# Odd mixer of a hybrid decoder step: four gate rows, and decay rows spread over the partitions by TensorE

## The chip, the cores and the metric

The kernel runs on one core of one Trainium2 chip. The metric is the device time of one execution in microseconds; lower is better. Three runs of the kernel before took 1924.58 to 1926.36 us, with a median of 1924.73 us.

## The reference, cut to what matters

Two decoder layers are applied to a prompt of 512 tokens and a sample group of 8 x 4 = 32 tokens, which share all weights (width 1024). Each layer is a SwiGLU half-step, a mixer and a second SwiGLU half-step. The change lies in the mixer of the second layer, a gated DeltaNet with 8 heads of width 128. Per head it does this (chunks of 64 tokens in the reference, of 128 in the kernel, which gives the same result):

```
q, k, v = silu(causal_conv(u @ w_in));  q, k = l2_normalize(q) * 128**-0.5, l2_normalize(k)
g = -exp(A_log) * softplus(a_logit + dt_bias);  G = cumsum(g)            # per head and token, within a chunk
decay = exp(where(s <= t, G[t] - G[s], -inf))                           # chunk x chunk
A = where(s < t, (k_t . k_s) * decay, 0) * beta_t;   P = (q_t . k_s) * decay
(I + A) [Uv, Wk] = [v * beta, k * beta * exp(G)]                        # unit lower triangular
for each chunk:  U = Uv - Wk S;  O = (q exp(G)) S + P U;  S = exp(G_last) S + (k exp(G_last - G))^T U
o = rms_norm(O, o_gain) * silu(z);   x = x + o @ w_out
```

The decay needs G twice: down the partitions (one value for each token of a row) and along the free axis, the same row of 128 values on every partition. The second form is what the change makes in another way. The "gate" is silu(z).

## The kernel before, in words

Activations are kept transposed: 8 tiles of 128 features x 544 tokens (512 of the prompt, 32 of the sample). A linear layer (`mm3`, L347) splits weights and activations each into a rounded part and a rest, and runs three matmuls for each 128 x 128 block of weights (L362 to L364), for the first 256 tokens and then for the other 288. One such pair of halves takes about 6 us of TensorE. Its results go to one of two PSUM buffers, in turn, and VectorE or another engine clears each before it can be used again.

In the odd mixer (L1499) the order of the work is written out by hand in `ODD_ORDER`: D decays of a group of two heads, H query and key of a head, B its values, V the triangular solve (62 small VectorE instructions, one after the other, L1223 and L1224), L the larger blocks of the inverse (`levels`), C the recurrence over the chunks (`chain`), S and R the sample group, Z a gate, O, M and U the output layer, N the convolution states:

```
ODD_ORDER = "D0 H0 H1 B0 B1 V0 Z0 L0 Z1 S0 C0 R0 D2 H2 B2 H3 B3 Z2 Z3 V2 L2 D4 S2 C2 R2 H4 H5 B5 D6 Z4 B4 V4 Z5 H6 S4 H7 B6 L4 V6 C4 R4 B7 Z6 O0 Z7 S6 N L6 C6 R6 M2 O6"
```

This order is a priority and not the final sequence: when the kernel is built, a planner puts the instructions of each engine into one fixed order, by that priority and its own estimate of when each is ready. It also hands out the buffers of each tile pool: a tile that finds all buffers of its tag taken waits for the last reader of one of them. On the chip every engine then works through its own list in order.

The steps that the change touches:

- `odd_setup` (L1008) computes G for all heads. It forms the cumulative sums by matmuls with constant matrices (L1042 to L1046), turns G on its side (`gt`, 40 rows x 128: row 8c+h is chunk c of head h, rows 32 to 39 are the sample's; L1072) and stores `gt` in DRAM (`gdr`, five DMAs, L1074 and L1075). The sample's rows come back on all 128 partitions in one DMA (`grs`, L1077).
- `head_decay` (L1128) loads a head's row of G on all partitions (`grow`, or `E.xsq` for the second head of a group; L1132) and makes the two decay matrices Dn and Dt, four VectorE instructions each (L1137, L1138), and their exponentials on ScalarE. `sample_decay` (L1351) does the same for the sample from `grs`.
- `head_stage` (L1146) transposes q and k into PSUM (tag "m", two buffers), squares each on ScalarE for the norms with the squares going to a scratch tile `E.junk` (L1158, L1164), copies k to the tile `kt` (L1165), makes A (L1177, into Dn) and P (L1184, into Dt), and stores A for the solve. `kt` is requested between the squares of q and the transposes of k.
- The tiles Dn, Dt, kt, qg and vb of all heads share the tag "st", which has 15 buffers: ten for a group of two heads.
- `chain` (L1281) and `sample_group` (L1368) also square into `E.junk` (L1335, L1383).
- `gate` (L1529) runs the linear layer of silu(z) for one head; VectorE clears it into a tile `sz` (L1537), which has three buffers. The gate is read when the chain ends (L1307, L370, L371).
- `odd_consts` (L969) loads the constant matrices during the FFN before the mixer.

Of the kernel before, what the change touches and what calls it, by code (L numbers as in the profile page):

```python
# [7 lines left out]
F32 = mybir.dt.float32  # L8
# [7 lines left out]
P = 128  # L16
D = 1024
T = 512
# [950 lines left out]
def odd_consts(E, op):  # L969
    nc, I = E.nc, E.I  # L970

    def const(key, shape):
        t = op.tile(shape, F32, name=key)
        nc.sync.dma_start(out=t, in_=I[key])
        return t
    E.tri = const("c_tri", [P, P])
    E.mba = const("c_mba", [P, P])
    E.mbp = const("c_mbp", [P, P])
    E.stri = const("c_stri", [NS, NS])
    E.sones = const("c_sones", [NS, NS])  # L980
    E.smba = const("c_smba", [NS, NS])
    E.smbp = const("c_smbp", [NS, NS])
    E.bsel = const("c_bsel", [96, DB])

    rows = E.f(P)[:96]
    nc.sync.dma_start(out=rows, in_=I["dn_conv_w"].rearrange("a i (k p) -> (a i k) p", p=P))
    ps = E.m([P, 96])
    nc.tensor.transpose(ps, rows, E.ident[:96, :96])
    E.cw = op.tile([P, 96], F32, name="cw")
    nc.vector.tensor_copy(E.cw, ps)  # L990
    E.cst = op.tile([P, 24, 27], F32, name="dncst")
    cv = I["state_dn_conv"].rearrange("a b i c -> (a b i) c")
    for g in range(6):
        st = E.f()
        nc.sync.dma_start(out=st[:24, :512], in_=cv[:, g * 512:(g + 1) * 512])
        ps = E.m([P, 4, 24])
        for j in range(4):
            nc.tensor.transpose(ps[:, j], st[:24, j * P:(j + 1) * P], E.ident[:24, :24])
        nc.vector.tensor_copy(E.cst[:, 4 * g:4 * g + 4, 3:], ps)
    gc = op.tile([P, 1], F32, name="ogain")  # L1000
    nc.sync.dma_start(out=gc, in_=I["dn_o_gain"].rearrange("a p -> p a"))
    E.ogain = gc
    E.ad = op.tile([P, 2, NH], F32, name="ad")
    nc.sync.dma_start(out=E.ad[:, 0], in_=I["dn_A_log"].to_broadcast([P, NH]))
    nc.sync.dma_start(out=E.ad[:, 1], in_=I["dn_dt_bias"].to_broadcast([P, NH]))


def odd_setup(E, op, sp, w_in):  # L1008
# [5 lines left out]
    def ev(h, c0, cn, ps):  # L1014
        nc.vector.tensor_tensor(bt[:16, c0:c0 + cn], ps[:16], E.rstd[:16, c0:c0 + cn], op=ALU.mult)
    mm3(E, [w], E.xh, E.xl, ev)
    ps = E.m([P, 5, 16])
    for t, (c0, n) in enumerate(TOKS):
        nc.tensor.transpose(ps[:n, t], bt[:16, c0:c0 + n], E.ident[:16, :16])
# [19 lines left out]
    nc.vector.tensor_tensor(gm, g[:NS, 4:5].to_broadcast([NS, DB, NH]), bc(E.bsel[:NS], NH), op=ALU.mult)  # L1039
    ps = E.m([P, 160])  # L1040
    gf = g[:, :4].rearrange("p a b -> p (a b)")
    nc.tensor.matmul(ps[:, 0:32], lhsT=E.tri, rhs=gf, start=True, stop=True)  # L1042
    nc.tensor.matmul(ps[:, 32:64], lhsT=E.ones, rhs=gf, start=True, stop=True)
    nc.tensor.matmul(ps[:NS, 64:72], lhsT=E.stri, rhs=g[:NS, 4], start=True, stop=True)
    nc.tensor.matmul(ps[:NS, 72:80], lhsT=E.sones, rhs=g[:NS, 4], start=True, stop=True)
    nc.tensor.matmul(ps[:, 96:160], lhsT=E.ones[:NS], rhs=gm.rearrange("p a b -> p (a b)"), start=True, stop=True)  # L1046
    E.G = op.tile([P, 5, NH], F32, name="G")
    nc.vector.memset(E.G, 0.0)
# [24 lines left out]
    for c in range(4):  # L1073
        nc.sync.dma_start(out=E.gdr[:, c * P:(c + 1) * P], in_=gt[8 * c:8 * c + 8, :P])  # L1074
    nc.sync.dma_start(out=E.gdr[:, T:], in_=gt[32:40, :NS])  # L1075
    E.grs = op.tile([P, NH, NS], F32, name="grs")
    nc.sync.dma_start(out=E.grs, in_=E.gdr[:, T:].unsqueeze(0).to_broadcast([P, NH, NS]))  # L1077


def conv_tile(E, op, w_in, i, h, sq):  # L1080
# [31 lines left out]
def ch(ap):  # L1112
    return ap[:, :T].rearrange("p (c t) -> p c t", c=4)


def cps(E, shape, tag="c"):
    return E.pm.tile(shape, F32, tag=tag, name=E.nm(tag))
# [10 lines left out]
def head_decay(E, op, h):  # L1128
    nc = E.nc
    H = Head()  # L1130
    grow = E.xsq if h % GH else op.tile([P, NT], F32, tag="grow", name=E.nm("grow"))
    nc.sync.dma_start(out=grow, in_=E.gdr[h:h + 1].to_broadcast([P, NT]))  # L1132
    Dn = op.tile([P, 4, P], F32, tag="st", name=E.nm("Dn"), bufs=ST)
    Dt = op.tile([P, 4, P], F32, tag="st", name=E.nm("Dt"), bufs=ST)
    for c in range(4):
        g = E.G[:, c, h:h + 1]
        nc.vector.scalar_tensor_tensor(Dn[:, c], ch(grow)[:, c], g, E.mba, op0=ALU.subtract, op1=ALU.max)  # L1137
        nc.vector.scalar_tensor_tensor(Dt[:, c], ch(grow)[:, c], g, E.mbp, op0=ALU.subtract, op1=ALU.min)  # L1138
    E.act(Dn, Dn, AF.Exp, scale=-1.0)
    E.act(Dt, Dt, AF.Exp)  # L1140
    E.act(grow[:, :T], grow[:, :T], AF.Exp)
    H.grow, H.A, H.PT = grow, Dn, Dt
    return H


def head_stage(E, op, w_in, h, H, ssq, adr, sq):  # L1146

    nc = E.nc
    gi = h % GH
    grow, A, PT = H.grow, H.A, H.PT  # L1150
    qT = conv_tile(E, op, w_in, 0, h, sq)
    kT = conv_tile(E, op, w_in, 1, h, sq)
    ssk = op.tile([P, 4], F32, tag="ssk", name=E.nm("ssk"), bufs=2)
    pq = E.m([P, 4, P])
    for c in range(4):
        nc.tensor.transpose(pq[:, c], ch(qT)[:, c], E.ident)
    for c in range(4):
        nc.scalar.activation(E.junk[0], pq[:, c], AF.Square, accum_out=ssq[:, gi, c:c + 1])  # L1158
    kt = op.tile([P, 4, P], F32, tag="st", name=E.nm("kt"), bufs=ST)
    pk = E.m([P, 4, P])  # L1160
    for c in range(4):
        nc.tensor.transpose(pk[:, c], ch(kT)[:, c], E.ident)
    for c in range(4):
        nc.scalar.activation(E.junk[0], pk[:, c], AF.Square, accum_out=ssk[:, c:c + 1])  # L1164
    nc.scalar.activation(kt, pk, AF.Copy)  # L1165
    nc.vector.tensor_scalar(ssk, ssk, EPS, None, op0=ALU.add)
    cf = op.tile([P, 4, 4], F32, tag="cf", name=E.nm("cf"), bufs=4)
    rk, rb, rb2, kwf = cf[:, 0], cf[:, 1], cf[:, 2], cf[:, 3]
    rsqrt_small(E, rk, ssk, [P, 4], "4")
    nc.vector.tensor_tensor(rb, rk, E.beta[:, :4, h], op=ALU.mult)  # L1170
    nc.vector.tensor_tensor(rb2, rb, rk, op=ALU.mult)
    nc.vector.scalar_tensor_tensor(kwf, rb2, -1.0, E.eG[:, :4, h], op0=ALU.mult, op1=ALU.mult)
    kk = E.m([P, 4, P])
    for c in range(4):
        nc.tensor.matmul(kk[:, c], lhsT=ch(kT)[:, c], rhs=ch(kT)[:, c], start=True, stop=True)
    for c in range(4):
        nc.vector.scalar_tensor_tensor(A[:, c], kk[:, c], rb2[:, c:c + 1], A[:, c], op0=ALU.mult, op1=ALU.mult)  # L1177
    for i in range(4):
        s = slice(32 * i, 32 * i + 32)
        nc.sync.dma_start(out=adr[i, gi].rearrange("c r s -> r c s"), in_=A[s, :, s])  # L1180
    qk = E.m([P, 4, P])
    for c in range(4):
        nc.tensor.matmul(qk[:, c], lhsT=ch(kT)[:, c], rhs=ch(qT)[:, c], start=True, stop=True)
    nc.vector.tensor_tensor(PT, qk, PT, op=ALU.mult)  # L1184
    qg = op.tile([P, 4, P], F32, tag="st", name=E.nm("qg"), bufs=ST)
    nc.gpsimd.tensor_tensor(qg, ch(qT), ch(grow), op=ALU.mult)
    kw = op.tile([P, 3, P], F32, tag="kw", name=E.nm("kw"), bufs=GH)
    for c in range(1, 4):
        nc.scalar.activation(kw[:, c - 1], kt[:, c], AF.Copy, scale=kwf[:, c:c + 1])
    for c in range(4):  # L1190
        nc.scalar.activation(kt[:, c], kt[:, c], AF.Copy, scale=E.egl[:, c, h:h + 1])
    H.qg, H.kg, H.kw, H.rb = qg, kt, kw, rb
# [88 lines left out]
def chain(E, op, Hs, V, g0, ssq, sz, yy, cuts=(4,)):  # L1281
# [29 lines left out]
    for c in range(4):  # L1311
# [20 lines left out]
            nc.tensor.matmul(po[:, h], lhsT=Hs[h].PT[:, c], rhs=U[:, h], start=(c == 0), stop=True)  # L1332
        nc.scalar.activation(ot[:, c], po, AF.Copy)
        for h in hs:
            nc.scalar.activation(E.junk[1], ot[:, c, h], AF.Square, accum_out=sso[:, h, c:c + 1])  # L1335
        S = Sn
        if c in cuts:
            finish(c - 4 // len(cuts), c)
# [29 lines left out]
def sample_group(E, op, sq, dec, g0, sz, yy):  # L1368
# [10 lines left out]
    nc.scalar.activation(kv, ps, AF.Copy)  # L1379
    kt, vt = kv[:, 0], kv[:, 1]  # L1380
    ssk = op.tile([NS, GH], F32, tag="sssk", name=E.nm("ssk"))
    for h in hs:
        nc.scalar.activation(E.junk[1][:NS], kt[:, h], AF.Square, accum_out=ssk[:, h:h + 1])  # L1383
    nc.vector.tensor_scalar(ssk, ssk, EPS, None, op0=ALU.add)
    cf = op.tile([NS, 4, GH], F32, tag="scf", name=E.nm("scf"))
    rk, rb, rb2, kwf = cf[:, 0], cf[:, 1], cf[:, 2], cf[:, 3]
# [26 lines left out]
        nc.tensor.matmul(pv[:, h], lhsT=A2[:, h], rhs=IB[:, h], start=True, stop=True)  # L1413
    V = R(NS, "V")
    nc.vector.tensor_tensor(V, pv, IB, op=ALU.add)
    kw = R(P, "kw")
    nc.vector.tensor_tensor(kw, kt, bc(kwf, P), op=ALU.mult)
    k3 = op.tile([96, GH, P], F32R, tag="k3", name=E.nm("k3"))
    for h in hs:
# [79 lines left out]
def odd_mixer(E, cp, w_in, w_out, nxt):  # L1499
    nc, tc = E.nc, E.tc  # L1500
    with E.phase(0, 2), tc.tile_pool(name=E.nm("oddw"), bufs=1) as op, tc.tile_pool(name=E.nm("odram"), bufs=1, space=bass.MemoryType.DRAM) as dp:
        E.dp, E.op = dp, op
        E.ft, E.rt = (op, "acc", XW, 4), (op, "y", YB)
        E.junk = [op.tile([P, P], F32, name=f"junk{i}") for i in range(2)]
        norm_stats(E)
        odd_setup(E, cp, op, w_in)
        odd_heads(E, op, dp, w_in, w_out, nxt)


def odd_heads(E, op, dp, w_in, w_out, nxt):  # L1510
# [156 lines left out]
```

## Time and profile before

| | us |
|---|---|
| median of the runs (lowest, highest) | 1924.73 (1924.58, 1926.36) |
| the profiled execution | 1924.04 |
| its span in the trace | 1922.3 |
| TensorE busy in the span | 1872.1 |
| VectorE busy | 1080.6 |
| ScalarE busy | 836.6 |
| GpSimd busy | 125.5 |

The profile follows one execution. A row of a timeline has the start in us from the span's start, the duration, the engine (PE TensorE, PEld its weight load, DVE VectorE, ACT ScalarE, POOL GpSimd, SPq the DMA queue of SyncE), the line of the kernel, the operation, output and inputs by tile name, the shape and how many instructions are merged; in brackets the idle time of that engine just before, and what ended it. One fp32 matmul of the kernel appears as two instructions, so "x8" of a 128x128 product are four matmuls. PEclk is the granted clock of TensorE as a share of full speed.

### The profile page before, as it was taken

How to read it: one execution, taken by the hardware profiler on the slowest of the kernel's cores; microseconds unless marked ns; L12 is line 12 of the kernel's file. 1: busy time of each engine (PE TensorE's matmuls, PEld its weight loads, DVE VectorE, ACT ScalarE, POOL GpSimd, SP SyncE). 2: the span in 40 equal slices, each digit the busy share in tenths (PEclk: the TensorE clock that was granted, in tenths of full speed). 3: DMA queues.
4: the chain of work that ended last, by engine and by line, in shares of the span. 5: the costliest groups of instructions: out<-in, count | busy, mean ns of one | idle time of the engine just before them, and what ended most of it. 6: DMA issues, size and time to landing. Idle time of an engine off the chain costs nothing.

```text
span 1922.3 us, 36590 instructions
## 1 busy us (share of the span) xinstructions
PE 1872.1 (97%) x15037; PEld 1792.7 (93%) x15037; DVE 1080.6 (56%) x2563; ACT 836.6 (44%) x1733; POOL 125.5 (7%) x237
## 2 busy tenths in 40 slices
PE   7999999999899999999999999899998999999999
PEld 7999999889768999999999999899998998999998
DVE  7444435786756544433544433688978877444422
ACT  6333324777744433322433322475775646333221
POOL 0000002111320000000000000112111100000000
PEclk9999999999999999999999999999999999999999
DMA  4333233322332333323333332333443332233232
GB/s 134 88 89 89 77 88 104 85 56 78 86 103 84 88 88 88 88 79 88 97 88 88 88 93 78 89 88 83 109 125 76 93 91 69 83 86 88 85 112 68
DMA packets 315972, 171.03 MB, mean 89 GB/s; under 512 B 28470, under 2 KB 310278, under 8 KB 315804
## 3 DMA queue, kind: packets, MB, share of 16 engines
q1 hardware_dynamic: 313244, 160.30, 29.7%
q0 software_dynamic: 2560, 8.39, 1.5%
q8 instruction: 118, 1.93, 0.4%
q14 instruction: 50, 0.41, 0.1%
HBM read 158.01 MB, written 10.65 MB: 88 GB/s over the span
## 4 chain that ended last, share of the span: by engine, by line
PE 84%; DVE 7%; ACT 4%; issue 2%; DMA 2%; POOL 1%; SPq 0%; ACTq 0%; DVEq 0%; POOLq 0%
PE lin L362 25%; PE lin L363 24%; PE lin L364 24%; PE pv L729 1%; DVE wl L324 1%; ACT wh L323 1%; PE sc L758 1%; PE po L805 1%; DMA raw<-in_w_ffn_in 1%; DVE acc L1106 1%; DVE LT L1224 1%; DVE ltmp L1223 1%; PE s L1451 0%; ACT f L100 0%; DMA raw<-in_w_in_odd 0%
## 5 line engine op out<-in xcount | busy, mean ns | idle before, releaser
L362 PE MATMUL lin<-xh,wh 128*128 128x256 f32 (+2 forms) x2992 | 873.8, 292 | 19.5 <-DVE sz L1537 4.5
L363 PE MATMUL lin<-xl,wh 128*128 128x256 f32 (+2 forms) x2992 | 871.1, 291 | 1.1 <-DVE xl L371 1.0
L364 PE MATMUL lin<-xh,wl 128*128 128x256 f32 (+2 forms) x2992 | 865.2, 289 | 0.8 <-DVE wl L324 0.8
L362 PEld LDWEIGHTS lin<-xh,wh 128*128 128x128 f32 (+1 forms) x2992 | 564.7, 189 | 26.7 <-ACT wh L323 8.4
L364 PEld LDWEIGHTS lin<-xh,wl 128*128 128x128 f32 (+1 forms) x2992 | 566.3, 189 | 6.1 <-issue 4.1
L363 PEld LDWEIGHTS lin<-xl,wh 128*128 128x128 f32 (+1 forms) x2992 | 564.9, 189 | 5.3 <-issue 1.7
L323 ACT ACTIVATE wh<-raw 128x1024 fp32r<-128x1024 f32 x261 | 275.8, 1057 | 493.3 <-PE lin L363 425.6
L324 DVE TENSOR_TENSOR wl<-raw,wh 128x1024 fp32r<-128x1024 f32 x261 | 317.4, 1216 | 89.5 <-PE lin L364 87.7
L362 PE MATMUL lin<-hh,wh 128*128 128x288 f32 (+1 forms) x1024 | 295.7, 289 | 0.0
L363 PE MATMUL lin<-hl,wh 128*128 128x288 f32 (+1 forms) x1024 | 295.4, 288 | 0.0
L364 PE MATMUL lin<-hh,wl 128*128 128x288 f32 (+1 forms) x1024 | 294.9, 288 | 0.0
L363 PEld LDWEIGHTS lin<-hl,wh 128*128 128x128 f32 x1024 | 193.0, 188 | 0.2
L364 PEld LDWEIGHTS lin<-hh,wl 128*128 128x128 f32 x1024 | 192.7, 188 | 0.1
L362 PEld LDWEIGHTS lin<-hh,wh 128*128 128x128 f32 x1024 | 192.5, 188 | 0.1
L401 DVE TENSOR_TENSOR sg<-lin,rstd 128x256 f32<-128x256 f32 (+1 forms) x128 | 55.9, 438 | 161.3 <-PE lin L364 161.3
L406 DVE TENSOR_TENSOR pr<-lin,rstd 128x256 f32<-128x256 f32 (+1 forms) x128 | 56.5, 441 | 155.3 <-PE lin L364 155.1
L370 ACT ACTIVATE hh<-pr 128x256 fp32r<-128x256 f32 (+1 forms) x128 | 55.1, 431 | 202.4 <-DVE pr L407 202.2
L423 DVE SCALAR_TENSOR_TENSOR x<-lin,x 128x256 f32<-128x256 f32 x64 | 28.2, 441 | 168.7 <-PE lin L364 168.7
L371 DVE TENSOR_TENSOR hl<-pr,hh 128x256 fp32r<-128x256 f32 (+1 forms) x128 | 56.6, 442 | 62.1 <-ACT hh L370 62.0
L100 ACT ACTIVATE sg<-sg 128x256 f32<-128x256 f32 (+1 forms) x128 | 53.7, 422 | 55.9 <-DVE sg L401 55.9
L267 ACT ACTIVATE xh<-x,vec 128x544 fp32r<-128x544 f32 (+2 forms) x64 | 39.6, 632 | 73.1 <-DVE x L423 59.3
L1106 DVE SCALAR_TENSOR_TENSOR acc<-XP,cw,acc 128x568 f32<-128x568 f32 x72 | 58.9, 818 | 2.1 <-ACT acc L1104 1.8
(480 smaller groups left out, 2091.3 us busy)
## 6 DMA issues: line engine op xcount, KB each, us to landing
raw<-in_w_ffn_in SPq DMA_DIRECT2D x128, 512.0 KB
raw<-in_w_ffn_out SPq DMA_DIRECT2D x64, 512.0 KB
raw<-in_w_in_odd SPq DMA_DIRECT2D x32, 512.0 KB
raw<-in_w_in_even SPq DMA_DIRECT2D x20, 512.0 KB
raw<-in_w_out_even SPq DMA_DIRECT2D x8, 512.0 KB
S<-in_state_dn_S SPq DMA_DIRECT2D x8, 512.0 KB
out_dn_S_sample<-S SPq DMA_DIRECT2D x8, 512.0 KB
raw<-in_w_out_odd SPq DMA_DIRECT2D x8, 512.0 KB
```

The lines of the kernel that those rows point to most:

```text
L100: i = self.nc.scalar.activation(out, in_, func, **kw).ins
L267: nc.scalar.activation(xh, x, AF.Copy, scale=g)
L323: nc.scalar.activation(self.h, raw, AF.Copy)
L324: nc.vector.tensor_tensor(self.l, raw, self.h.bitcast(F32), op=ALU.subtract)
L362: nc.tensor.matmul(ps[:n], lhsT=wh, rhs=rh, start=(i == 0), stop=False)
L363: nc.tensor.matmul(ps[:n], lhsT=wh, rhs=rl, start=False, stop=False)
L364: nc.tensor.matmul(ps[:n], lhsT=wl, rhs=rh, start=False, stop=(i == len(terms) - 1))
L370: nc.scalar.activation(yh, src, AF.Copy)
L371: nc.vector.tensor_tensor(yl, src, yh.bitcast(F32), op=ALU.subtract)
L401: nc.vector.tensor_tensor(s, ps, E.rstd[:, c0:c0 + cn], op=ALU.mult)
L406: nc.vector.tensor_tensor(p_, ps, E.rstd[:, c0:c0 + cn], op=ALU.mult)
L1106: nc.vector.scalar_tensor_tensor(a, XP[:, j:j + XW - 3], cw[j], a, op0=ALU.mult, op1=ALU.add)
```

## The change

Four things are done. The sample's rows of G (`grs`) and the two rows of heads 0 and 1 are spread over the partitions by TensorE: a matmul whose weights are one column of the identity, repeated 128 times, copies one row of `gt` to all partitions. The other heads still load theirs from DRAM. The gates get four buffers in place of three. The scratch tile `E.junk` is gone: squares go to `kt` in `head_stage` (which is therefore requested before the transposes of q), to `vb` in `chain` and to `kw` in `sample_group`. Three constant matrices are loaded in `odd_setup`, into a work tile, and no longer kept from the FFN on.

```diff
 def odd_consts(E, op):
-    E.tri = const("c_tri", [P, P])
-    E.stri = const("c_stri", [NS, NS])
-    E.sones = const("c_sones", [NS, NS])
 def odd_setup(E, op, sp, w_in):
     mm3(E, [w], E.xh, E.xl, ev)
+    cst = E.f()
+    tri, stri, sones = cst[:, :P], cst[:NS, P:P + NS], cst[:NS, P + NS:P + 2 * NS]
+    for t, key in ((tri, "c_tri"), (stri, "c_stri"), (sones, "c_sones")):
+        nc.sync.dma_start(out=t, in_=E.I[key])
...
     nc.sync.dma_start(out=E.gdr[:, T:], in_=gt[32:40, :NS])
     E.grs = op.tile([P, NH, NS], F32, name="grs")
-    nc.sync.dma_start(out=E.grs, in_=E.gdr[:, T:].unsqueeze(0).to_broadcast([P, NH, NS]))
+    row = lambda r: E.ident[:40, r:r + 1].to_broadcast([40, P])
+    ps = cps(E, [P, NH, NS], "s")
+    for h in range(NH):
+        nc.tensor.matmul(ps[:, h], lhsT=row(32 + h), rhs=gt[:40, :NS], start=True, stop=True)
+    nc.scalar.activation(E.grs, ps, AF.Copy)
+    E.growps = [cps(E, [P, 4, P], t) for t in ("c", "z")]
+    for h, ps in enumerate(E.growps):
+        for c in range(4):
+            nc.tensor.matmul(ps[:, c], lhsT=row(8 * c + h), rhs=gt[:40, :P], start=True, stop=True)
 def head_decay(E, op, h):
-    nc.sync.dma_start(out=grow, in_=E.gdr[h:h + 1].to_broadcast([P, NT]))
+    if h < GH:
+        src = E.growps[h]
+    else:
+        nc.sync.dma_start(out=grow, in_=E.gdr[h:h + 1].to_broadcast([P, NT]))
+        src = ch(grow)
...
-        nc.vector.scalar_tensor_tensor(Dn[:, c], ch(grow)[:, c], g, E.mba, op0=ALU.subtract, op1=ALU.max)
-        nc.vector.scalar_tensor_tensor(Dt[:, c], ch(grow)[:, c], g, E.mbp, op0=ALU.subtract, op1=ALU.min)
+        nc.vector.scalar_tensor_tensor(Dn[:, c], src[:, c], g, E.mba, op0=ALU.subtract, op1=ALU.max)
+        nc.vector.scalar_tensor_tensor(Dt[:, c], src[:, c], g, E.mbp, op0=ALU.subtract, op1=ALU.min)
-    E.act(grow[:, :T], grow[:, :T], AF.Exp)
+    E.act(ch(grow), src, AF.Exp)
 def head_stage(E, op, w_in, h, H, ssq, adr, sq):
+    kt = op.tile([P, 4, P], F32, tag="st", name=E.nm("kt"), bufs=ST)
     pq = E.m([P, 4, P])
...
-        nc.scalar.activation(E.junk[0], pq[:, c], AF.Square, accum_out=ssq[:, gi, c:c + 1])
-    kt = op.tile([P, 4, P], F32, tag="st", name=E.nm("kt"), bufs=ST)
+        nc.scalar.activation(kt[:, c], pq[:, c], AF.Square, accum_out=ssq[:, gi, c:c + 1])
...
-        nc.scalar.activation(E.junk[0], pk[:, c], AF.Square, accum_out=ssk[:, c:c + 1])
+        nc.scalar.activation(kt[:, c], pk[:, c], AF.Square, accum_out=ssk[:, c:c + 1])
 def chain(E, op, Hs, V, g0, ssq, sz, yy, cuts=(4,)):
-            nc.scalar.activation(E.junk[1], ot[:, c, h], AF.Square, accum_out=sso[:, h, c:c + 1])
+            nc.scalar.activation(Hs[h].vb[:, c], ot[:, c, h], AF.Square, accum_out=sso[:, h, c:c + 1])
 def sample_group(E, op, sq, dec, g0, sz, yy):
+    kw = R(P, "kw")
     for h in hs:
-        nc.scalar.activation(E.junk[1][:NS], kt[:, h], AF.Square, accum_out=ssk[:, h:h + 1])
+        nc.scalar.activation(kw[:, h], kt[:, h], AF.Square, accum_out=ssk[:, h:h + 1])
...
-    kw = R(P, "kw")
 def odd_mixer(E, cp, w_in, w_out, nxt):
-        E.junk = [op.tile([P, P], F32, name=f"junk{i}") for i in range(2)]
     def gate(h):
-        z = op.tile([P, NT], F32, tag="sz", name=E.nm("sz"), bufs=3)
+        z = op.tile([P, NT], F32, tag="sz", name=E.nm("sz"), bufs=4)
```

The matmuls of L1042 to L1045 take `tri`, `stri` and `sones` in place of `E.tri`, `E.stri` and `E.sones`.

## Rows read from the trace of the kernel before

**Rows 1.** Busy time by stretch: the odd mixer (span us, then engines busy, PEclk, DMA).

```profile
1200.00:1640.00 440.00, 418.81 (x3888) 391.65 (x3887) 354.17 (x1231) 269.42 (x760) 61.60 (x128) 0.98 0.35 92
```

**Rows 2.** Timeline of VectorE, first decays.

```profile
1229.44 0.28 DVE L1072 COPY gt<-m 40x128 f32<-40x128 f32 x1 [0.39 <-PE m L1070]
...
1237.83 0.35 DVE L1137 SCALAR_TENSOR_TENSOR Dn<-grow,G,c_mba 128x128 f32<-128x128 f32 x1 [0.25 <-DMA grow<-gdr]
...
1242.76 0.42 DVE L1092 TENSOR_TENSOR XP<-lin,rstd 128x256 f32<-128x256 f32 x1
```

**Rows 3.** Timeline of TensorE, the stretch after.

```profile
1243.32 0.36 PE L362 MATMUL lin<-xh,wh 128*128 128x256 f32 x1 [2.68 <-DVE XP L1092]
```

**Rows 4.** Busy time by stretch after two stalls of TensorE (PEclk is third from last).

```profile
1243.30:1247.20 3.90, 3.88 (x20) 3.90 (x21) 2.69 (x8) 3.35 (x7) 3.09 (x5) 0.58 0.12 22
1452.90:1458.90 6.00, 6.00 (x28) 6.00 (x29) 5.07 (x19) 2.05 (x8) 0.00 (x0) 0.50 0.33 90
```

**Rows 5.** Timeline of TensorE: fp32 matmuls between linear ones, in two places.

```profile
1250.30 1.16 PE L1175 MATMUL m<-acc 128*128 128x128 f32 x8
1251.21 0.38 PE L364 MATMUL lin<-xh,wl 128*128 128x288 f32 x1
...
1490.92 0.40 PE L1464 MATMUL s<-ident,uo 32*128 32x32 f32 x2
1491.16 0.38 PE L1465 MATMUL s<-sPT,Us 32*128 32x32 f32 x2
```

**Rows 6.** Groups of VectorE by line and form: output, input, count, busy us, mean ns.

```profile
L1177 DVE SCALAR_TENSOR_TENSOR Dn<-m,cf,Dn 128x128 f32<-128x128 f32 x32 | 9.1, 343 | 0.0
...
L1137 DVE SCALAR_TENSOR_TENSOR Dn<-xsq,G,c_mba 128x128 f32<-128x128 f32 x16 | 5.5, 346 | 0.6 <-DMA xsq<-gdr 0.6
```

**Rows 7.** Timeline of ScalarE and of SyncE's DMA queue, first decays.

```profile
1235.27 0.77 ACT L1104 ACTIVATE acc<-XP,cw 128x568 f32<-128x568 f32 x1 [5.17 <-DVE XP L1096]
...
1213.24 0.35 SPq L1215 DMA_DIRECT2D LT<-in_c_lid  x1
```

**Rows 8.** Timeline of VectorE and TensorE around the sixth gate.

```profile
1448.71 0.68 DVE L371 TENSOR_TENSOR y<-sz,y 128x512 fp32r<-128x512 f32 x1
...
1452.42 0.41 DVE L1537 TENSOR_TENSOR sz<-lin,rstd 128x256 f32<-128x256 f32 x1
...
1452.89 0.58 PE L362 MATMUL lin<-xh,wh 128*128 128x256 f32 x1 [4.50 <-DVE sz L1537]
```

**Rows 9.** Timeline of ScalarE, keys of heads 7 and 3 (of head 7, first and last square).

```profile
1497.62 0.28 ACT L1164 ACTIVATE junk<-m 128x128 f32<-128x128 f32 x1 [0.70 <-PE m L1162]
...
1499.00 0.19 ACT L1164 ACTIVATION_READ_ACCUMULATOR junk<-m 128x1 f32 x1
...
1510.68 0.60 ACT L1165 ACTIVATE kt<-m 128x512 f32<-128x512 f32 x1 [1.11 <-PE c L1270]
...
1350.64 0.59 ACT L1165 ACTIVATE kt<-m 128x512 f32<-128x512 f32 x1
```

**Rows 10.** Timeline of VectorE: head 3's norm, A of head 7, starts of two solves.

```profile
1337.08 0.15 DVE L956 TENSOR_SCALAR rsi<-ssk 128x4 int32<-128x4 int32 x1
...
1339.73 0.15 DVE L961 SCALAR_TENSOR_TENSOR cf<-rsa,rsy 128x4 f32<-128x4 f32 x1
...
1361.53 0.20 DVE L1223 TENSOR_TENSOR ltmp<-LA,LT 128x31 f32<-128x31 f32 x1
...
1507.12 1.13 DVE L1177 SCALAR_TENSOR_TENSOR Dn<-m,cf,Dn 128x128 f32<-128x128 f32 x4
...
1523.39 0.20 DVE L1223 TENSOR_TENSOR ltmp<-LA,LT 128x31 f32<-128x31 f32 x1
```

**Rows 11.** Timeline of SyncE's DMA queue and TensorE: two solves back, last levels.

```profile
1474.76 2.16 SPq L1242 DMA_DIRECT2D V<-tdr  x4
...
1560.22 2.61 SPq L1242 DMA_DIRECT2D V<-tdr  x4
...
1571.66 0.24 PE L1248 MATMUL c<-ident,V 32*32 32x32 f32 x2
```

More of the change, by code (lines that the diff above doesn't have):

```diff
@@ L1041, in odd_setup @@
     gf = g[:, :4].rearrange("p a b -> p (a b)")
-    nc.tensor.matmul(ps[:, 0:32], lhsT=E.tri, rhs=gf, start=True, stop=True)
+    nc.tensor.matmul(ps[:, 0:32], lhsT=tri, rhs=gf, start=True, stop=True)
     nc.tensor.matmul(ps[:, 32:64], lhsT=E.ones, rhs=gf, start=True, stop=True)
-    nc.tensor.matmul(ps[:NS, 64:72], lhsT=E.stri, rhs=g[:NS, 4], start=True, stop=True)
-    nc.tensor.matmul(ps[:NS, 72:80], lhsT=E.sones, rhs=g[:NS, 4], start=True, stop=True)
+    nc.tensor.matmul(ps[:NS, 64:72], lhsT=stri, rhs=g[:NS, 4], start=True, stop=True)
+    nc.tensor.matmul(ps[:NS, 72:80], lhsT=sones, rhs=g[:NS, 4], start=True, stop=True)
     nc.tensor.matmul(ps[:, 96:160], lhsT=E.ones[:NS], rhs=gm.rearrange("p a b -> p (a b)"), start=True, stop=True)
```

## The prediction

> **What bounds the kernel now.** I read the busy times by stretch first. In the odd mixer, the only part whose work the change touches, TensorE is busy for 418.8 of 440 us and VectorE for 354.2 [rows 1]. So TensorE sets the pace, VectorE is close behind, and a change pays only by what it takes from TensorE's idle time or by bringing back its clock. The timeline of TensorE then shows which of its stalls the change can reach: there are two.
>
> The first stands at the first decays. `gt` is ready at 1229.72 (1229.44 + 0.28), but VectorE starts Dn at 1237.83, after the way through DRAM, 8.1 us later [rows 2]. The sixteen Dn and Dt instructions then run as one block, and behind them waits the clearing of a linear result, at 1242.76. TensorE has filled both linear buffers by then and stands idle for 2.68 us [rows 3]. [...]
>
> The second stands at the sixth gate (Z5). Its tile `sz` is the third of three buffers, and it is taken until the chain of the second group has read it: L371 at 1448.71, done at 1449.39. Its clearing comes at 1452.42, TensorE idles for 4.50 us [rows 8], and for the 6.0 us after that the clock is 0.50 [rows 4], another 3.0 us lost. Together 7.5 us, the larger of the two.
>
> **The change part by part.** *Rows by TensorE.* Added are 8 matmuls for `grs` and 8 for two `grow`, all fp32, with weights of 128 columns. Four fp32 products of 128x128 take 1251.21 - 1250.30 = 0.91 us from the first to the next linear matmul, 0.23 each; a product with 32 columns behind weights of 128 takes 1491.16 - 1490.92 = 0.24 [rows 5]. So 16 x 0.23 = **3.7 us** of TensorE, wherever they land, since it is never without work here except in the stall. In exchange the 8.1 us through DRAM fall to the 12 products that head 0 waits for, 2.8 us. VectorE is then asked for its sixteen instructions at about 1233, when TensorE, held up by its 3.7 us, has most of head 0's key projection (6 us, two halves) ahead of it. The block takes at most 1242.76 - 1237.83 = 4.9 us [rows 2] and ends by 1238, so the first half's clearing comes before TensorE wants that buffer for the half after next. I see no stall left there, and without it no lower clock: -4.3 + 3.7 = **-0.6 us**. The bounds: nothing regained but the matmuls paid, +3.7; all regained and half of the matmuls in idle time, -2.5.
>
> VectorE now reads the rows from PSUM. [...]
>
> *Edits that cost nothing.* ScalarE copies `grs` out of PSUM; it idles 5.17 us there [rows 7]. The queue of SyncE has three transfers fewer behind `gt` and three small ones (the constants) more, about 1 us by the 0.35 us of a similar one [rows 7]; the next weights may be issued that much later, which two tiles of weights in hand cover. If that cover is gone, it costs the 1 us. The squares written to `vb` make ScalarE wait for nothing new, because the recurrence has read `vb` by then; but they hold that buffer some 2 to 4 us longer at the end of each chain, and Dn of the next group waits for such buffers. Other tiles of the same chain come free first, so I put it at 0, with the 2 to 4 us as the upper bound.
>
> *The fourth gate buffer.* With it Z5 takes the buffer of the second gate, which the first chain has long read. The second half is ready when the idle time begins, 1452.89 - 4.50 = 1448.4, the first half 3 us earlier, and each can be cleared about then. TensorE goes on with the next linear work, whose weights are split by then. VectorE is busy (5.07 of 6.0 us even behind the stall [rows 4]), so the second clearing may still come at 1452.4: TensorE then has 3 us of the next half to do, and could wait for 1 us. I take **-7.5 us**; bounds -7.5 and, if VectorE is the brake anyway, 0.
>
> *The earlier request for `kt`.* This edit speaks against the change. Fifteen "st" buffers are ten for a group, four for the Dn and Dt of the next, and one for its first `kt`: at the second head of every later group (3, 5, 7) all are taken. Before, that cost little: head 7's key squares ran from 1497.62 to 1499.19, and only the copy into `kt` waited, until 1510.68, for `levels` (L1270) to give back a buffer; head 3's copy came at 1350.64 [rows 9]. Now the squares of q are the first to write `kt`, so all squares, the norm, A and the solve wait as well. For head 7: 1510.68, plus eight squares 3.2 us (four took 1.6), plus the norm 2.7 (eleven small instructions, 1337.08 to 1339.88), plus A 1.1, is 1517.6, where A ended at 1508.25 [rows 10]: 9.4 us later. If the norm is as delayed as it was (9.1 us from 1499.19 to 1508.25) it is 14.7 later. The last solve starts that much later than 1523.39. It had slack: the transfers of its result are issued until 1562.8 and `levels` begins at 1571.66 [rows 11], 8.8 us later; I take 2.0 of that for the landing (an estimate: a quarter of the 8.1 us above, which hold two issues and two landings), so 6.8 are slack. So 9.4 - 6.8 = **+2.6 us** lands on the end of the mixer, where only the output layer is left to fill TensorE; bounds 0 (the way from A to the solve has slack too) and 14.7 - 6.8 = 7.9. Head 3: A at about 1357.5; through DRAM as above (8.1) 1365.6, where its solve began at 1361.53, 4.1 late. There three gates and two heads of linear work stand ready, so I take 0; the bounds are 0 and 11.4, by which A itself is late.
>
> **Sum:** -0.6 - 7.5 + 2.6 = -5.5 us. The sum is made against the profiled execution, 1924.04 us (span 1922.3 and 1.7 around it), 0.7 below the median of 1924.73. Against the median it is **1919.2 us**.
>
> **The rivals.** *All of it (1916.6 us).* `kt` costs nothing, because `levels` of the third group, which gives back the buffer, moves up in TensorE's order; its solve was on its way back by 1477, over 30 us before the buffer came free [rows 9, 11]. -8.1. Against it: that place is the planner's.
> *Taken back at the end (1924.5 us).* Head 7 is late by its upper bound, +7.9, and the gain is gone: -0.2. For it: VectorE is 80% busy in the mixer [rows 1], and chains of small instructions stretch.
> *The gate's clearing stays late (1926.7 us).* The change then doesn't do what it says: the planner puts the clearing behind the chain's instructions, which come first by priority, and only -0.6 + 2.6 = +2.0 remains. For it: even after the release at 1449.39 the clearing came only 3.0 us later [rows 8]. Against it: those 3 us are a backlog that the stall itself let in.
> *Slower (1932 us).* The buffer wait decides at every second head: head 3 pays the middle of its bounds, 7.7 us, and head 7 its 7.9, so -8.1 + 15.6 = +7.5. It decides from the point where TensorE runs out of linear work that may go ahead: both "m" buffers in PSUM hold q and k of the waiting head until the squares are done, so no other head's transposes get in. For it: head 7's wait was 11.5 us long already [rows 9]. Against it: 24 us of gates and projections can be moved into the first of them.
>
> **How the numbers follow.** Chances: forecast 0.35, all of it 0.16, taken back 0.20, clearing late 0.10, slower 0.19. About 0.2% (3.85 us) is what a measurement of this kernel can tell from no change. Faster are the first two, 0.51, rounded to 0.50; the same are the two in the middle, 0.31; slower 0.19. The range goes from 2 us below "all of it" (half of the new matmuls in idle time), 1914.5, up to 1930.0, which takes in both middle cases and the lower part of the slow one; some 0.18 is left out. The likeliest case by itself: 1916.6 to 1921.
>
> **What would show it.** Dn of head 0 should start near 1233 with no DMA before it, and TensorE should have no idle time above 1 us there. The wait of 4.50 us on `sz` L1537 should be gone, and PEclk 1.00 after it. Rows of L1158 for heads 3, 5 and 7 should stand after L1270 or L1331 of the group before; the last solve should start later against `levels` of the third group, and more idle time of TensorE should stand between the last `levels` and the end of the mixer. I am wrong if a stall at the first decays remains, if TensorE idles between heads 2 and 5, or if `kt` gets its buffer without a wait.

## The result, and the profile after

The changed kernel takes **1949.71 us** (median of 6 runs, 1943.44 to 1953.89) against 1924.65 (1923.31 to 1927.57) for the kernel before on the same chip: a ratio of 1.0124, 95% interval [1.0111, 1.0137]. It is slower by 25 us where I forecast 5.5 us faster. The profiled execution took 1951.0 us (span 1949.2).

Line numbers have moved: the clearings L1092 and L1537 are L1102 and L1550, the squares of q and k L1173 and L1178, A is L1191, `levels` begins at L1262. The first decays in the timelines of TensorE and VectorE, and the granted clock around them (busy time by stretch; PEclk is third from last):

```profile
1232.70 1.97 PE L1082 MATMUL s<-gt,ident 40*128 40x32 f32 x16
1234.51 1.27 PE L1087 MATMUL c<-gt,ident 40*128 40x128 f32 x8
1235.57 1.91 PE L1087 MATMUL z<-gt,ident 40*128 40x128 f32 x8
...
1248.77 0.92 PE L1171 MATMUL m<-ident,acc 128*128 128x128 f32 x4 [1.88 <-ACT acc L100]
```

```profile
1232.11 0.28 DVE L1073 COPY gt<-m 40x128 f32<-40x128 f32 x1 [0.38 <-PE m L1071]
...
1235.82 0.35 DVE L1151 SCALAR_TENSOR_TENSOR Dn<-c,G,c_mba 128x128 f32<-128x128 f32 x1
```

```profile
1232.00:1235.00 3.00, 3.00 (x27) 2.87 (x26) 2.25 (x4) 0.71 (x4) 0.00 (x0) 1.00 0.03 6
1235.00:1238.00 3.00, 3.00 (x16) 2.78 (x16) 2.80 (x13) 1.00 (x5) 0.30 (x1) 0.56 0.63 175
1238.00:1241.00 3.00, 3.00 (x15) 3.00 (x15) 3.00 (x10) 1.39 (x3) 0.00 (x0) 0.50 0.00 0
```

Dn starts 3.7 us after `gt` and no longer 8.4 [rows 2], and TensorE's wait of 2.68 us [rows 3] is gone. In its place stand 4.7 us of products, a lower clock from about their last quarter on (1.00 of full speed from 1232 to 1235, 0.69 in the us behind that, 0.50 from 1236 to 1242) with no idle time of TensorE in these rows (3.00 of 3.00 us busy), and a new wait of 1.88 us for the silu of a convolution on ScalarE. The sixth gate and the last group, in the timelines of TensorE, VectorE and ScalarE:

```profile
1463.53 1.35 PE L1317 MATMUL c<-ident,ot 128*128 128x128 f32 x4 [2.04 <-ACT ot L1314]
...
1465.82 1.09 PE L1317 MATMUL c<-ident,ot 128*128 128x128 f32 x4 [0.94 <-DVE sz L1321]
...
1468.63 0.58 PE L362 MATMUL lin<-xh,wh 128*128 128x256 f32 x1 [1.73 <-DVE sz L1550]
...
1506.04 0.60 PE L1171 MATMUL m<-ident,acc 128*128 128x128 f32 x4
...
1600.99 0.25 PE L1262 MATMUL c<-ident,V 32*32 32x32 f32 x4
```

```profile
1530.02 0.28 ACT L1173 ACTIVATE kt<-m 128x128 f32<-128x128 f32 x1
```

```profile
1537.71 1.11 DVE L1191 SCALAR_TENSOR_TENSOR Dn<-m,cf,Dn 128x128 f32<-128x128 f32 x4
```

The 4.50 us of [rows 8] are now three waits of 4.7 us together. Head 7's q is transposed at 1506.04 and squared only at 1530.02; its A comes at 1537.71 where it came at 1507.12 [rows 10], and the last `levels` at 1600.99 where they began at 1571.66 [rows 11].

**What TensorE lost.** The table is worked out from busy time by stretch, one profile each, in stretches of 20 us from 1180 to 1680: idle is 20 less the busy time, the clock's part is busy time times (1 - PEclk). A is the start of A (L1177 before) in VectorE's timeline. The first column names the runs that the next section tells of.

| kernel | A of head 3 | head 5 | head 7 | lost to 1540 | lost from 1540 | median us | ratio to before [95%] |
|---|---|---|---|---|---|---|---|
| before | 1342.5 | 1411.7 | 1507.1 | 22.6 | 4.4 | 1924.65 | |
| sz_j1 | 1344.8 | 1416.2 | 1498.4 | 17.6 | 6.0 | 1922.21 | 0.9978 [0.9968, 0.9987] |
| all_j1_rows1 | 1346.7 | 1416.5 | 1498.7 | 15.8 | 5.9 | 1924.27 | 0.9989 [0.9979, 0.9999] |
| rows_h3 | 1335.8 | 1418.9 | 1501.1 | 16.3 | 6.9 | 1927.04 | 1.0006 [0.9996, 1.0016] |
| kt7_sz | 1349.0 | 1419.4 | 1519.8 | 22.9 | 14.4 | 1927.53 | 1.0007 [0.9995, 1.0019] |
| all_j1_h3 | 1334.9 | 1420.4 | 1503.2 | 18.4 | 6.8 | 1928.44 | 1.0012 [1.0002, 1.0022] |
| rows128_h3 | 1337.1 | 1423.3 | 1505.5 | 17.6 | 7.3 | 1928.93 | 1.0011 [1.0002, 1.0020] |
| kt5_sz | 1341.8 | 1437.2 | 1506.8 | 20.5 | 15.0 | 1932.27 | 1.0031 [1.0020, 1.0043] |
| kt3_sz | 1358.7 | 1416.3 | 1509.4 | 19.9 | 15.1 | 1934.51 | 1.0042 [1.0026, 1.0057] |
| before_flip | 1359.2 | 1415.0 | 1513.4 | 26.7 | 4.7 | 1935.12 | 1.0051 [1.0036, 1.0066] |
| sz_pq | 1366.7 | 1424.0 | 1518.3 | 32.6 | 10.1 | 1936.44 | 1.0048 [1.0031, 1.0065] |
| all_j1 | 1362.9 | 1418.6 | 1514.1 | 23.3 | 15.3 | 1936.85 | 1.0056 [1.0042, 1.0070] |
| before_h3 | 1335.2 | 1439.4 | 1516.6 | 30.4 | 8.8 | 1936.93 | 1.0049 [1.0033, 1.0065] |
| kt_early | 1360.1 | 1442.8 | 1523.6 | 26.5 | 10.7 | 1937.69 | 1.0060 [1.0047, 1.0073] |
| after_pq | 1364.2 | 1426.3 | 1521.7 | 26.8 | 8.8 | 1941.02 | 1.0071 [1.0058, 1.0084] |
| after_h3 | 1359.5 | 1448.6 | 1527.9 | 24.7 | 11.2 | 1942.79 | 1.0090 [1.0075, 1.0106] |
| rows_only | 1366.0 | 1421.6 | 1519.2 | 32.1 | 14.6 | 1944.68 | 1.0089 [1.0076, 1.0102] |
| after | 1369.4 | 1460.3 | 1537.7 | 34.1 | 12.7 | 1949.71 | 1.0124 [1.0111, 1.0137] |

From before to after TensorE lost 19.8 us more; with 3.7 us of new products and the 2.7 us by which this profile reached the mixer later (1221.1 for 1218.4; the profiles spread from 1218.2 to 1222.7 there, ahead of every edit but three small loads, and the starts in the table carry that with them) that is 26.2 of the 27.0 us between the two profiled executions.

### The profile page after: what moved, and what is told of

Read it like the earlier page. It is cut to its first block, busy times and chain, and to the rows that moved or that the text cites. A ratio compares the mean times of both kernels' runs of the same rounds, so it can differ in the third digit from the quotient of the medians.

```text
span 1949.2 us, 36656 instructions
## 1 busy us (share of the span) xinstructions
PE 1890.5 (97%) x15069; PEld 1808.2 (93%) x15069; DVE 1076.8 (55%) x2563; ACT 832.3 (43%) x1734; POOL 125.3 (6%) x237
## 4 chain that ended last, share of the span: by engine, by line
PE 83%; DVE 9%; ACT 4%; DMA 2%; issue 1%; POOL 1%; SPq 0%; ACTq 0%; DVEq 0%; POOLq 0%
PE lin L362 24%; PE lin L364 24%; PE lin L363 24%; DVE wl L324 1%; DVE acc L1116 1%; PE pv L729 1%; DMA raw<-in_w_in_odd 1%; PE sc L758 1%; PE po L805 1%; ACT wh L323 1%; DMA raw<-in_w_ffn_in 1%; DVE LT L1238 1%; DMA S<-in_state_dn_S 1%; DVE ltmp L1237 1%; PE c L1335 0%
## 5 line engine op out<-in xcount | busy, mean ns | idle before, releaser
L323 ACT ACTIVATE wh<-raw 128x1024 fp32r<-128x1024 f32 x261 | 276.0, 1057 | 512.3 <-PE lin L363 433.3
```

Source lines behind the costliest of these rows:

```text
L323: nc.scalar.activation(self.h, raw, AF.Copy)
```

## The experiments

The medians of before ran from 1925.46 to 1926.23 in the four sets of runs, each on a chip of its own; differences below are of medians, so up to 0.8 us of one between two sets is before's own, and the ratios with their intervals stand in the table. **First: each part alone, and the change without the early `kt`.** kt_early takes only the edits that drop `junk`; rows_only only the products. sz_pq and after_pq keep `kt` late by squaring into PSUM:

```diff
-        nc.scalar.activation(E.junk[0], pq[:, c], AF.Square, ...)
+        nc.scalar.activation(pq[:, c], pq[:, c], AF.Square, ...)
-        nc.scalar.activation(E.junk[0], pk[:, c], AF.Square, ...)
+        nc.scalar.activation(pq[:, c], pk[:, c], AF.Square, ...)
```

kt_early: 

> The kernel before with one edit: the squares of q and k go into kt (asked for before the squares), those of the outputs into vb, those of the sample keys into kw; three gate buffers and the way through DRAM stay. Theory K (the early request for kt costs most of the 25 us): in the changed kernel A of heads 3, 5 and 7 is 27, 49 and 31 us later than before, and the losses at 1340 to 1400 and in the tail come to about 17 us; so about 1941 us, with the q squares of head 3 some 30 us behind their transposes. Rival R (the rows by TensorE cost it, and what is late later is only their 7 to 10 us passed on): within 3 us of 1924.7, and A of heads 3, 5, 7 within 10 us of before.

rows_only: 

> The kernel before with one edit: the rows of the first group and of the sample by TensorE; junk tiles, three gate buffers and resident constants stay. From the changed trace: 4.7 us of products, 3.2 us lost to a lower granted clock behind them, less the 4.3 us of the stall that they remove, and 2 to 3 us more of a later wait: theory K says about 1924.7 + 7 = 1931 us, with the clock near 0.5 in the 5 us behind the products. Rival R says the whole 25 us, about 1949 us. My own forecast's -0.6 would be 1924.

sz_pq: 

> The kernel before with the fourth gate buffer, room for it by loading the three constants into a temporary tile and by no junk tiles; but the squares of q and k are written in PSUM (into pq, already read), so kt is asked for as late as before. The forecast's step (the stall of 4.5 us at the sixth gate and its 3 us of lower clock go) gives 1924.7 - 7.5 = 1917 us. If the gate's clearing stays late because it stands behind the chain in VectorE's order: within 3 us of 1924.7.

after_pq: 

> The changed kernel with one edit: the squares of q and k are written in PSUM (into pq, already read), so kt is asked for as late as before; rows by TensorE, four gate buffers and the squares into vb and kw stay. Theory K: the 17 us of the kt wait come back, about 1949.7 - 17 = 1933 us, and A of heads 3, 5, 7 is within 12 us of its place before. Rival R: about 1949 us.

All four were slower than before: by 11.7, 18.7, 10.5 and 15.0 us. Theory K was near for kt_early, far off for the others, and the parts do not add up to the 25.1 of the whole. The two PSUM controls were spoilt: they hold one of the two "m" buffers for longer, and head 3's key transposes start at 1347.13 in sz_pq (1334.87 in sz_j1, below). What the four have in common is the first column of the table: A of head 3 is 18 to 24 us late. In rows_only, where no buffer is asked for earlier, ScalarE's timeline shows how. Three of head 3's four key squares (the first and the second are shown) stand behind the second `U` of the first chain, and in the kernel before they were done at 1335.7, ahead of it:

```profile
1346.28 0.27 ACT L1176 ACTIVATE junk<-m 128x128 f32<-128x128 f32 x1
...
1348.38 0.37 ACT L1330 ACTIVATE U<-z 128x256 f32<-128x256 f32 x1
...
1352.52 0.37 ACT L1330 ACTIVATE U<-z 128x256 f32<-128x256 f32 x1
...
1355.32 0.27 ACT L1176 ACTIVATE junk<-m 128x128 f32<-128x128 f32 x1
```

That order is fixed when the kernel is built, by priorities and due times, so the products had moved it. This is theory F (the flip).

**Second: the fourth buffer alone, and the flip undone.** sz_j1 keeps one junk tile, for which two small setup tiles move into `bt`'s; `_h3` changes one word of the order:

```diff
+        E.junk = [op.tile([P, P], F32, name="junk0")]
-    ba = op.tile([P, 5, 16], F32, name="ba")
+    ba = btv[:, NT:NT + 80].rearrange("p (a b) -> p a b", a=5)
-ODD_ORDER = "... D2 H2 B2 H3 B3 Z2 ..."
+ODD_ORDER = "... D2 H2 H3 B2 B3 Z2 ..."
```

sz_j1: 

> The kernel before with the fourth gate buffer alone: one junk tile for the heads (so kt is asked for as late as before), squares of the outputs into vb and of the sample keys into kw, the three constants in a temporary tile and two small setup tiles in a tile that is free then. Its order on ScalarE is nearly that of before: the squares of head 3's keys stand ahead of the first chain. The forecast's step: the stall at the sixth gate goes with its lower clock, 1925 - 7.5 = 1917.5. Theory F (what cost the earlier runs their time is that the squares of head 3's keys fell behind the first chain in ScalarE's order): no flip here, so 1917 to 1925. Rival (any edit costs 10 or more against an order that was tuned): about 1936, as the run with the squares in PSUM.

rows_h3: 

> Rows by TensorE alone, with one word of the hand-written order changed: head 3 ahead of the values of head 2 (H2 H3 B2 B3 for H2 B2 H3 B3), which puts the squares of head 3's keys ahead of the first chain again. Theory F: A of head 3 comes near 1351 (8 us behind before) and not at 1366, the second solve starts near 1370, and of the 18.7 us that the rows alone cost some 10 come back: 1932 to 1936. Rival (the rows cost it by their products and the clock, the flip costs nothing): within 3 us of 1944.7.

all_j1_h3: 

> The changed kernel without its early request for kt (one junk tile for the heads, kept room for as in the run with the fourth buffer alone) and with head 3 ahead of the values of head 2 in the hand-written order. Theory F with K: rows +7, fourth buffer 0 to -7.5, no flip and no wait for kt: 1925 to 1932. Rival (rows and order cost the same whatever stands where): about 1941 to 1949.

before_h3: 

> The kernel before with the one word of the order changed and nothing else: a control. If the word is worth something by itself and not only where the flip had happened, this is faster or slower than before by over 4 us; theory F says within 4 us of 1925, since head 3's keys were already ahead of the first chain.

sz_j1 is faster than before, by 3.5 us. The products with the flip undone cost 1.3 us, not 18.7 (what the word itself is worth in that order is in the figure): A of head 3 is back at 1335.8. The whole change without the early `kt` comes to 1928.4. The control missed: the word alone costs before 11.2 us (ratio 1.0049). Its A of head 3 is early, but that of head 5 is 27.7 us late. So theory F had to be widened: it is not that one place, but **whichever second head of a group comes late**. The table agrees over all runs, with limits drawn after they were in: where A of head 3 comes at 1358 or later, or A of head 5 at 1437 or later, the kernel takes over 1932 us, and where neither does, under 1929. Head 7 does not sort them: in kt7_sz its A is 21 us later than in sz_j1, and the time is 1927.5.

**Third: the early `kt` with the flip undone, the flip without it, and two other forms of the products.** all_j1 is all_j1_h3 with the old word. rows128_h3 and all_j1_rows1 change how the rows are made:

```diff
-    row = lambda r: E.ident[:40, r:r + 1].to_broadcast([40, P])
+    row = lambda r: E.ident[:, r:r + 1].to_broadcast([P, P])
```

```diff
+        nc.vector.tensor_tensor(gx, gt[:40, :P].unsqueeze(1).to_broadcast([40, 4, P]), m40[:, :4, h:h + 1].to_broadcast([40, 4, P]), op=ALU.mult)
+        nc.tensor.matmul(ps.rearrange("p c t -> p (c t)"), lhsT=E.ones[:40], rhs=s, start=True, stop=True)
```

after_h3: 

> The changed kernel with only the one word of the order changed (H2 H3 B2 B3); its early request for kt stays. Against the run without the early request (1928.4, same word) it prices the wait for kt alone. Theory K: the buffer, not the order, holds the squares of heads 3, 5 and 7, so A of these heads is 15 to 40 us later than there, and the time is 1940 to 1946. Rival F2 (the wait cost only by way of the order at head 3, which the word mends): 1928 to 1932.

all_j1: 

> The changed kernel without the early request for kt (one junk tile for the heads) and with the order's words as they were. Its squares of head 3's keys fall behind the first chain in ScalarE's order. Theory F: the flip costs here what it cost the rows alone (1944.7 - 1927.0 = 17.6), so about 1942 to 1946, with A of head 3 near 1366. Rival (the flip matters only together with other things, as the control's 9 us for the word alone suggest): 1928 to 1933.

rows128_h3: 

> Rows by TensorE with the word changed, each product over 128 rows (88 of them zeros) instead of 40; the order on every engine is that of the run with 40 rows. Theory C (the granted clock falls behind the products because few of the array's rows work): the clock stays near 1.00 from 1233 to 1239, where it was 0.66 and 0.77, and the next heads are 1.5 us earlier: 1925.5. Rival (it falls because the array waits for a full set of weights before each short product): the same fall and 1927 within 2.

all_j1_rows1: 

> The changed kernel without the early request for kt, with its words of the order as they were, and with the rows made by three products behind one set of weights (ones; VectorE first writes each row into its own columns, zeros elsewhere) instead of sixteen behind sixteen sets. ScalarE's order is close to that of the kernel before. If the sixteen loads of weights are what cost TensorE its 4.7 us and its clock there: no fall of the clock at 1233 to 1239, and against the fourth buffer alone (1922.2) the stall at the first decays is gained: 1918 to 1920. Rival (the rows gain nothing however they are made, the next wait takes it): 1922 to 1924. If the order turns out against it: 1930 or more.

The early `kt` costs 14.4 us with the word (1942.8 - 1928.4) and 12.9 without (1949.7 - 1936.9): theory K holds, and F2 falls. The flip costs 8.4 us in all_j1 (1936.9 - 1928.4), below the 14 to 18 that I had expected there. The two forms of the products gained nothing in time. Three products behind one set of weights leave TensorE 1.40 us of idle time at 1239.42, and the clock, 1.00 from 1237 to 1240, is 0.53 and 0.50 in the two stretches of 3 us behind that; against sz_j1 (1922.2) they are 2.1 us behind and not ahead. The 128-row form is told of at the end.

**Fourth: the lateness alone, and head by head.** before_flip only forces the place of four squares; kt7_sz, kt3_sz and kt5_sz are sz_j1 with the early request at one head:

```diff
+        if h == 3:
+            E.after(i.ins, E.first_u)
```

```diff
+    early = h in (7,)
+    kt = op.tile([P, 4, P], F32, tag="st", name=E.nm("kt"), bufs=ST) if early else None
+    sqo = lambda c: kt[:, c] if early else E.junk[0]
```

before_flip: 

> The kernel before with one forced order and no other edit: on ScalarE the squares of head 3's keys may only follow the second U of the first chain, the place that they have in the changed kernel and with the rows alone. Theory F: A of head 3 moves from 1342 to about 1362, the second solve and levels 10 to 20 us later, and the time is 1925.7 + 8 to 17: 1934 to 1942. Rival (what the rows cost lies in other shifts of the order): within 3 us of 1925.7.

kt7_sz: 

> The kernel with the fourth gate buffer alone (1922.2), with kt asked for early, and its squares written there, at head 7 only; the order is the same up to head 6. The forecast's term: +2.6 (bounds 0 and 7.9), so 1925 (1922 to 1930). Theory T (nothing but the output layer stands behind the last group, and the last solve has less slack than the 6.8 us that I gave it): +10 or more, 1932 to 1936, with A of head 7 over 15 us later and the end later by nearly as much as the last levels.

kt3_sz: 

> The same with the early request at head 3 only. The forecast's term: 0 (bounds 0 and 11.4), 1922. By the loss of the changed kernel between 1340 and 1400 (4 to 6 us): 1926 to 1928. If it acts like the flip of the order, which it contains (the squares of head 3 wait until the first chain's buffers come free): 8 or more, 1930 to 1936.

kt5_sz: 

> The same with the early request at head 5 only. The forecast gave it nothing, 1922. In the changed kernel A of head 5 was the latest of all (49 us behind before). If that lateness is covered by the linear work of heads 6 and 7 and the gates: 1922 to 1924. If it passes on to the third solve and from there to the last group: 1927 to 1932. The three heads together should come to the 12.9 us between the changed kernel and the same without the early request.

Forcing the place of four small squares costs the kernel before 9.7 us, with no work added; the planner orders the rest anew around them, and that is in the price. Against sz_j1 the early request costs 12.3 us at head 3, 10.1 at head 5 and 5.3 at head 7. Together that is 27.7 where the three cost 12.9 in place, so they overlap. That a group which is late already is not made late again would explain it; no run shows it. In kt7_sz ScalarE's timeline has the wait as forecast: the buffer comes from `levels` of the third group.

```profile
1511.82 0.28 ACT L1163 ACTIVATE kt<-m 128x128 f32<-128x128 f32 x1 [0.87 <-PE c L1275]
...
1514.10 0.61 ACT L1170 ACTIVATE kt<-m 128x512 f32<-128x512 f32 x1
```

Where the time is lost is seen in the tail. These are stretches of sz_j1, then of kt5_sz:

```profile
1540.00:1560.00 20.00, 20.00 (x157) 18.44 (x156) 18.07 (x66) 8.50 (x19) 1.80 (x2) 1.00 0.28 72
1560.00:1580.00 20.00, 20.00 (x304) 17.71 (x303) 12.12 (x44) 9.51 (x28) 0.39 (x1) 1.00 0.33 95
1580.00:1600.00 20.00, 19.57 (x167) 18.04 (x166) 10.58 (x35) 9.39 (x33) 0.00 (x0) 1.00 0.29 81
```

```profile
1540.00:1560.00 20.00, 18.11 (x125) 16.22 (x124) 17.36 (x68) 7.53 (x18) 1.48 (x2) 0.87 0.17 43
1560.00:1580.00 20.00, 18.78 (x287) 15.97 (x285) 9.42 (x38) 7.92 (x23) 0.57 (x1) 0.96 0.25 70
1580.00:1600.00 20.00, 19.53 (x142) 17.66 (x143) 10.18 (x32) 8.23 (x26) 0.00 (x0) 0.83 0.35 106
```

In kt5_sz the last `levels` start only 0.7 us later than in sz_j1 (1570.9 and 1570.2; 3.6 counted from the start of the mixer), yet from 1540 on TensorE loses 15.0 us and not 6.0: idle time (1.9, 1.2 and 0.5 us in the three stretches), and the clock (0.87, 0.96 and 0.83 there, 1.00 in sz_j1). kt3_sz loses 15.1 there. That the tail loses the time is shown; how a wait near 1350 or 1430 leads to it is not. One reading would be that the linear work which filled the wait is missing later. The traces speak against it: of the 288 matmuls of the output layer on `y`, sz_j1 has run 262 by 1590, kt5_sz 213 and kt3_sz 203, so more linear work is left there and not less. In kt5_sz TensorE stands idle in front of such a matmul, because VectorE has not made the rest `wl` of its weights. VectorE makes it 3.8 us later than in sz_j1, though the rounded part starts at nearly the same time in both (L323 of ScalarE at 1543.73 and 1544.11). TensorE and VectorE of kt5_sz, then VectorE of sz_j1:

```profile
1554.85 0.56 PE L364 MATMUL lin<-y,wl 128*128 128x256 f32 x1 [0.82 <-DVE wl L324]
...
1553.60 1.20 DVE L324 TENSOR_TENSOR wl<-raw,wh 128x1024 fp32r<-128x1024 f32 x1
```

```profile
1549.82 1.21 DVE L324 TENSOR_TENSOR wl<-raw,wh 128x1024 fp32r<-128x1024 f32 x1
```

VectorE is busy up to both, so it is its order that differs. The same wait of 0.82 us stands in kt3_sz, at 1557.45. The planner makes a new order for each edit: of some 1210 instructions of VectorE from 1225 to 1640, 1008 keep their order from sz_j1 to kt5_sz, 927 from sz_j1 to kt3_sz and 1069 from before to before_flip (counted by operation and tile; 1198 from rows_h3 to rows128_h3). Each price above is thus that of an edit together with the order that the build makes of it, and no run parts the two.

before_flip is another case: it loses in the stretches before 1540 (26.7 for 22.6), and its profiled execution, 1930.5 us, lies 4.7 below its median, so the table shows too little of it (that of kt7_sz lies 7.4 above, so there it shows too much).

## Why the prediction was wrong, step by step

*Early request for `kt`: the wait right, its cost wrong, and this is the first of two steps that failed.* "Head 3: ... I take 0" because "three gates and two heads of linear work stand ready": measured alone, 12.3 us. For head 5 I named the wait and gave it no term: 10.1. For head 7 I took 2.6 with bounds 0 and 7.9: 5.3, inside the bounds by luck, since the 6.8 us of slack that I took off are not there. From the start of the last solve to the first `levels` behind it the kernel before takes 48.3 us, sz_j1 48.6 and kt7_sz 50.7: a late solve has nothing to make up for it with, so in kt7_sz these `levels` come 13.2 us later than in sz_j1 (1583.4 for 1570.2), and the kernel still loses only 5.3. In place the three cost 12.9 to 14.4. The cover of head 3 was real: from 1260 to 1400 TensorE loses 5.0 us in kt3_sz and 6.0 in sz_j1. The loss stands from 1540 on (15.1 for 6.0), where I did not look for it. My rival "Slower (1932 us)" had this wait at every second head, with 15.6 us; I gave it 0.19. It prices heads 3 and 7 and leaves out 5, and its 7.7 is not the middle of the bounds 0 and 11.4, which is 5.7 and would put the rival at 1930.

*Rows by TensorE, -0.6.* The 4.3 us in it are the wait of 2.68 us [rows 3] and 3.9 us at a granted clock of 0.58 [rows 4], 3.9 x 0.42 = 1.6. The products took what I said (3.8 us in rows_h3, from 1230.26 on), VectorE started when I said (1233.24 there), the DRAM way and the stall of 2.68 us went. But the lower clock came back behind the products (0.66 and 0.77 in the 6 us from 1233 in rows_h3, 1.7 us lost), and a new wait of 1.88 us stood further on, so in rows_h3 the first `levels` are 3.4 us later (1326.4 for 1323.0), near the bound of +3.7. Over the whole kernel it is 1.3 us (ratio 1.0006 [0.9996, 1.0016]). The second step that failed is one that I did not have at all: in the changed kernel the products also moved the fixed order of the squares, and with it they cost 14.6 us (1936.9 - 1922.2). My sum treats the order of before as given.

*VectorE reading PSUM: right.* The sum has no term for it. Before, the same kind of instruction took 343 ns with a PSUM operand (L1177) and 346 ns without (L1137) [rows 6]; in the changed kernel Dn from PSUM takes 0.35 and 0.34 us.

*Fourth gate buffer, -7.5: right in its place.* Busy time by stretch, before and then sz_j1:

```profile
1440.00:1460.00 20.00, 14.25 (x91) 13.50 (x90) 18.09 (x65) 12.09 (x27) 2.05 (x6) 0.83 0.24 66
```

```profile
1440.00:1460.00 20.00, 19.30 (x152) 18.65 (x151) 19.27 (x71) 13.87 (x30) 2.36 (x8) 1.00 0.49 129
```

Before lost 20 - 14.25 x 0.83 = 8.2 us here and sz_j1 0.7, a gain of 7.5. But 3.5 is what the run gained (with the edits that I put at nothing, the constants and the squares to `vb` and `kw`, which no run prices by themselves): sz_j1 loses more from 1260 to 1400 (6.0 for 3.9) and from 1540 on (6.0 for 4.4). In the changed kernel nothing of it is left, since the second solve is late (1383.39 for 1361.53) and its chain with it: the clearing (L1550 at 1468.16) stands among the chain's instructions in VectorE's order, as in my rival "The gate's clearing stays late".

*Ladder.* Fourth buffer with those edits -3.5 (1922.2), rows with their order +14.6 (1936.9), early `kt` +12.9 (1949.7): 24.0 of the 25.1 us; the rest is before's median between the sets.

*Of "what would show it":* the stall at the first decays changed its waiter instead of going; the squares of heads 3, 5 and 7 did wait; the last solve did move, by 27.2 us (1550.55 for 1523.39).

The best version is sz_j1, 0.22% faster than before and 1.4% than the change: the fourth buffer, with the squares of q and k kept out of `kt`.

## What to carry to other kernels

An edit that makes a chain late must be priced over the whole kernel, and not only by whether other work fills the wait: here the wait was filled, and the loss stood more than 100 us later. Where an order is fixed at build, look in the trace for which short instructions won their place narrowly (here four squares of 0.28 us ahead of a chain), because an edit upstream can turn them, and measure an edit together with a control that puts them back. Before a scratch tile is saved by writing to a result's buffer early, ask when that buffer comes free.

## What I had not expected of the hardware

The granted clock fell here without idle time. Seven kernels have the sixteen products over 40 rows. In the four of them with stretches of 3 us it fell late in the products or just behind them: to 0.56 and 0.50 in the changed kernel, 0.66 and 0.77 in rows_h3 and after_pq, 0.50 in after_h3, with TensorE busy for 3.00 of 3.00 us in each, as the profile counts it. For the other three (rows_only, all_j1, all_j1_h3) there is one stretch of 20 us, from 1220 to 1240, with 0.80, 0.77 and 0.83 where before has 0.91. With the same order on every engine and 128 rows (zeros in 88) it stayed at 1.00. Busy time by stretch, first rows_h3, then rows128_h3, whose products run about 3 us later (1233.46):

```profile
1230.00:1233.00 3.00, 3.00 (x27) 2.87 (x27) 2.22 (x6) 0.88 (x3) 0.00 (x0) 1.00 0.03 6
1233.00:1236.00 3.00, 3.00 (x19) 2.86 (x19) 3.00 (x14) 1.23 (x4) 0.30 (x1) 0.66 0.71 175
1236.00:1239.00 3.00, 3.00 (x20) 3.00 (x20) 3.00 (x9) 0.81 (x2) 0.00 (x0) 0.77 0.00 0
```

```profile
1233.00:1236.00 3.00, 3.00 (x29) 3.00 (x28) 2.46 (x6) 0.86 (x4) 0.00 (x0) 1.00 0.03 6
1236.00:1239.00 3.00, 3.00 (x27) 3.00 (x26) 3.00 (x14) 1.16 (x5) 0.30 (x1) 1.00 0.70 174
1239.00:1242.00 3.00, 2.93 (x23) 2.72 (x22) 3.00 (x10) 1.31 (x3) 0.00 (x0) 1.00 0.00 0
```

The 1.7 us that this saves (3 x 0.34 + 3 x 0.23) are not seen in the times (1928.9 and 1927.0, intervals overlapping), and it is one profile of the 128-row form, so that the 40 rows are the cause stays likely and not settled.

The changed kernel's own time spreads over 10.4 us in its six runs, against 4.3 for before beside it; in the other sets before spreads over 4.4 to 8.5.
